# The last six inner tiles of a feed-forward's way out: four as seven half-size products in eight PSUM banks, two added onto them

## The chip, the cores and the metric

One core of a Trainium2 chip runs the kernel; the whole program is one launch. The metric is the device time of one execution in microseconds, taken as the median of several runs.

## The reference

Two layers, each a feed-forward half-step, a token mixer and a second feed-forward half-step, over 512 tokens of 1024 features in float32. The change touches the feed-forward alone. `D_FF` is 2816, which is 22 tiles of 128.

```python
def swiglu(h, w_in, w_out):
    gate, up = jnp.split(h @ w_in, 2, axis=-1)
    return (jax.nn.silu(gate) * up) @ w_out

for l in range(DEPTH):
    x = x + 0.5 * swiglu(rms_norm(x, ffn1_norm[l]), ffn1_w_in[l], ffn1_w_out[l])
    h = rms_norm(x, mix_norm[l]) @ w_mix_in[l]
    ...                      # short convolution, HGRN2, forgetting attention
    x = x + y @ w_mix_out[l]
    x = x + 0.5 * swiglu(rms_norm(x, ffn2_norm[l]), ffn2_w_in[l], ffn2_w_out[l])
```

## The kernel before

**Precision.** Every float32 product is made of three TensorE passes over `fp32r` parts: ScalarE casts the high part of an operand, VectorE subtracts it from the source for the low part, and `mm3` issues high x high, high x low, low x high. Weights go through `prepare`: ACT writes `hi` (L810), DVE writes `lo` (L812), into a buffer `hl` of which there are three. `prepare` for a step is issued `LEAD` = 3 steps before it. The moving operand is split the same way: `two`, called by `moving` for the way out (ACT L759 or L763, DVE L760 or L764; tiles `m`).

**Half-size products.** The activations stay transposed: features or inner tiles on the partitions, 512 tokens in the free dimension, cut in two halves of 256. A product of a 2x2-blocked weight with a 2x2-blocked activation is made from seven products of blocks instead of eight (P1 to P7, a scheme of the Strassen-Winograd family). Its left operands are blocks of weights and sums of blocks (S1 to S4, made by `add` and `adds`, accumulating DMAs on POOL's queue, and by `total` on DVE), its right operands blocks and sums of blocks of the activation (`SUM`, `hidden`). One product is `product()`: 24 matmuls of 128x128 weights against 256 columns into one PSUM bank.

**Way in and way out.** The way in ("I" steps) makes two inner tiles from seven products: gate and up, then SiLU on ACT, and a product on DVE into `hq`, a quarter of the hidden activation. The way out ("O" steps) takes eight inner tiles (a chunk) at a time: `CHUNKS` are tiles 0 to 7, 8 to 15 and 16 to 21. Both are woven together: `plan()` writes the order of steps `seq` from patterns of I and O, and for each step a list of jobs with ranks: loads on SP's queue, accumulations on POOL's, sums on DVE, moving operands. `halved()` runs that order; after a step's matmuls come its readout, the `prepare` of the step three further on, and the step's jobs. An engine works its instructions off in the order in which they are issued.

**The last chunk.** It goes out directly, without products: `hh` and `hl` hold the hidden tiles 16 to 21 as high and low parts (ACT L973, DVE L974), and after `halved()` the loop in `ffn` (L489 to L507) streams `w_out`'s rows against all 512 tokens, four banks for features 0 to 511 and then four for 512 to 1023: 144 matmuls of 512 columns. `stream` loads and casts those weights (`st`, L314 and L315). DVE adds each bank to the residual `xT` (L502), and `norm_part` gathers what the next norm needs (x times gain at L408 and L409, squares at L421 and L425). The fourth and last feed-forward has another end, `way_out`, which writes the output.

**PSUM.** Eight banks: `mm` 3, `sc` 2, `pt` 2, `po` 1, in two rings of four that the I steps and O steps take in turn; the rings swap at each feed-forward (`ntog`).

Of the kernel before, what the change touches and what calls it, by code (L numbers as in the profile page):

```python
# [62 lines left out]
def plan(covered):  # L63
# [5 lines left out]
    for c, pattern in ((0, "IIIIO" + "IIO" * 11 + "IOIO"), (1, "IIIIO" + "IOIIO" * 5 + "IOIOO")):  # L69
        ii, oo = iter(into(CHUNKS[c + 1])), iter(outof(c))  # L70
        seq += [next(ii if k == "I" else oo) for k in pattern]
        assert next(ii, None) is None and next(oo, None) is None
# [53 lines left out]
    for b, e, u, q in sorted(lives, key=lambda x: x[0]):  # L126
# [33 lines left out]
class Trunk:  # L160
# [297 lines left out]
    def ffn(self, w_in, w_out, next_gain, covered, begin=None, out=None):  # L458
        nc = self.nc
        tc = self.tc  # L460
        with tc.tile_pool(name=self.n("ffn"), bufs=1) as fp:
# [18 lines left out]

            f0, nf = CHUNKS[-1]
            if next_gain is not None:
                self.begin_norm(next_gain)
# [4 lines left out]
            for dg in range(2):
                banks = self.next4()  # L489

                def parts(k, kk, dg=dg):
                    r = slice((f0 + k) * P, (f0 + k + kk) * P)
                    return [w_out[r, dg * 512 : (dg + 1) * 512]]

                self.stream(
                    [(bk, slice(c, c + P), None) for bk, c in zip(banks, (0, 128, 256, 384))],
                    parts, self.last_hidden, nf,
                )
                for i in range(4):
                    j = dg * 4 + i  # L500
                    xj = self.xT[:, j, :]
                    nc.vector.scalar_tensor_tensor(  # L502
                        out=xj, in0=banks[i], scalar=0.5, in1=xj,
                        op0=ALU.mult, op1=ALU.add,
                    )
# [1417 lines left out]
```

## Time and profile before

| | us |
|---|---|
| median of 3 runs (lowest 1802.62, highest 1804.36) | 1803.07 |
| the profiled execution | 1801.38 |
| its span in the trace | 1799.6 |
| TensorE busy | 1792.0 |
| VectorE busy | 1430.1 |
| ScalarE busy | 1001.0 |
| GpSimd busy | 176.6 |

The profile is of one execution. A row of groups reads: line, engine, operation, output<-inputs with the shape of the tile, count | busy time, mean ns of one | idle time before them and what ended it. A row of the timeline reads: start in us from the span's start, duration, engine, line, operation, and in brackets the idle time before it with what ended it. Buffer numbers are left out of names.

### The profile page before, as it was taken

The page shows a single profiled execution, that of the slowest core. Times are in us where ns is not written, and L with a number is a line of the kernel's source. Part 1 is how long each engine was busy: PE and PEld are TensorE (multiplying, and loading weights), DVE is VectorE, ACT ScalarE, POOL GpSimd, SP SyncE. Part 2 cuts the span into 40 slices and gives each one's busy share as a digit, 9 for nine tenths or more (in the row PEclk, how much of TensorE's full clock was granted, in tenths as well). Part 3 has the DMA queues.
Part 4 walks back from the last instruction along what each step waited for, and adds up shares of the span by engine and source line. Part 5 has one row for each costly group of instructions (what it writes and reads, how often), then busy time and mean ns, then how long its engine had stood idle before and what let it go on. Part 6 is the DMA issues. An engine that isn't in the chain of part 4 may idle for free.

```text
span 1799.6 us, 34747 instructions
## 1 busy us (share of the span) xinstructions
PE 1792.0 (100%) x14271; PEld 1681.0 (93%) x14271; DVE 1430.1 (79%) x2006; ACT 1001.0 (56%) x1445; POOL 176.6 (10%) x184
## 2 busy tenths in 40 slices
PE   9999999999999999999999999999999999999999
PEld 7899999899888899999889999998998888999997
DVE  9889787676888798879679887876868879888793
ACT  5455554464776465556446555555547755555551
POOL 0011120100000002112001111201000000020210
PEclk9999999999999999999999999999999999999999
DMA  7659793233433857868265786913334346597762
GB/s 207 180 133 196 169 188 97 71 82 84 106 98 108 222 130 170 194 163 166 82 207 133 169 185 175 187 65 83 78 85 116 89 144 179 141 185 190 160 133 94
DMA packets 244638, 254.09 MB, mean 141 GB/s; under 512 B 18904, under 2 KB 228576, under 8 KB 244480
## 3 DMA queue, kind: packets, MB, share of 16 engines
q1 hardware_dynamic: 189424, 182.38, 33.7%
q0 software_dynamic: 54752, 69.23, 23.8%
q8 instruction: 112, 1.84, 0.4%
q14 instruction: 46, 0.38, 0.1%
q10 hardware_dynamic: 304, 0.27, 0.0%
HBM read 223.98 MB, written 2.10 MB: 126 GB/s over the span
## 4 chain that ended last, share of the span: by engine, by line
PE 94%; DVE 2%; ACT 2%; DMA 1%; issue 1%; SPq 0%; POOL 0%; ACTq 0%; DVEq 0%; POOLq 0%
PE mm L328 14%; PE mm L336 14%; PE mm L337 14%; PE sc L328 6%; PE sc L336 6%; PE sc L337 6%; PE pt L336 6%; PE pt L328 6%; PE pt L337 6%; PE po L328 4%; PE po L336 4%; PE po L337 4%; PE po L1654 1%; PE pt L1698 1%; PE pt L1352 1%
## 5 line engine op out<-in xcount | busy, mean ns | idle before, releaser
L810 ACT CAST hl<-w 128x1024 fp32r<-128x1024 f32 x322 | 336.8, 1050 | 305.9 <-PE mm L337 80.4
L812 DVE TENSOR_TENSOR hl<-w,hl 128x1024 fp32r<-128x1024 f32 x322 | 391.8, 1220 | 96.7 <-ACT hl L810 96.7
L315 DVE TENSOR_TENSOR hl<-st,hl 128x512 fp32r<-128x512 f32 (+3 forms) x196 | 162.5, 830 | 116.2 <-ACT hl L314 115.0
L314 ACT CAST hl<-st 128x512 fp32r<-128x512 f32 (+3 forms) x196 | 143.1, 732 | 174.3 <-PE po L337 66.8
L328 PE MATMUL mm<-xc,hl 128*128 128x256 f32 (+1 forms) x733 | 201.3, 276 | 0.0
L336 PE MATMUL mm<-xc,hl 128*128 128x256 f32 x728 | 201.2, 276 | 0.0
L337 PE MATMUL mm<-xc,hl 128*128 128x256 f32 x728 | 201.0, 276 | 0.0
L328 PE MATMUL sc<-xc,hl 128*128 128x256 f32 (+1 forms) x532 | 146.0, 276 | 0.0
L336 PE MATMUL sc<-xc,hl 128*128 128x256 f32 x528 | 146.0, 276 | 0.0
L337 PE MATMUL sc<-xc,hl 128*128 128x256 f32 x528 | 145.8, 276 | 0.0
L328 PEld LDWEIGHTS mm<-xc,hl 128*128 128x128 f32 x733 | 137.4, 188 | 0.2
L337 PEld LDWEIGHTS mm<-xc,hl 128*128 128x128 f32 x728 | 136.7, 188 | 0.0
L336 PEld LDWEIGHTS mm<-xc,hl 128*128 128x128 f32 x728 | 136.7, 188 | 0.0
L328 PE MATMUL pt<-xc,hl 128*128 128x256 f32 (+1 forms) x482 | 132.6, 276 | 0.0
L336 PE MATMUL pt<-xc,hl 128*128 128x256 f32 x480 | 132.6, 276 | 0.0
L337 PE MATMUL pt<-xc,hl 128*128 128x256 f32 x480 | 132.5, 276 | 0.0
L328 PE MATMUL mm<-x,hl 128*128 128x512 f32 x272 | 107.6, 396 | 0.0
L336 PE MATMUL mm<-x,hl 128*128 128x512 f32 x272 | 106.3, 391 | 0.0
L337 PE MATMUL mm<-x,hl 128*128 128x512 f32 x272 | 106.2, 390 | 0.0
L328 PEld LDWEIGHTS sc<-xc,hl 128*128 128x128 f32 x532 | 99.7, 188 | 0.2
L336 PEld LDWEIGHTS sc<-xc,hl 128*128 128x128 f32 x528 | 99.1, 188 | 0.0
L337 PEld LDWEIGHTS sc<-xc,hl 128*128 128x128 f32 x528 | 99.1, 188 | 0.0
(517 smaller groups left out, 5575.0 us busy)
## 6 DMA issues: line engine op xcount, KB each, us to landing
w<-in_ffn_w_in_dram SPq DMA_DIRECT2D x140, 512.0 KB, 5.1
w<-in_ffn_w_out_dram SPq DMA_DIRECT2D x64, 512.0 KB, 5.2
w<-in_ffn_w_out_dram POOLq DMA_DIRECT2D x56, 512.0 KB, 7.2
st<-in_w_mix_in_dram SPq DMA_DIRECT2D x88, 256.0 KB, 2.8
st<-in_ffn_w_in_dram SPq DMA_DIRECT2D x70, 256.0 KB, 3.1
w<-in_ffn_w_in_dram POOLq DMA_DIRECT2D x35, 512.0 KB, 8.9
w<-S POOLq DMA_DIRECT2D x35, 512.0 KB, 4.7
st<-in_ffn_w_out_dram SPq DMA_DIRECT2D x24, 512.0 KB, 5.3
```

The source lines that it names most:

```text
L314: a = nc.scalar.copy(hi, src[:, c : c + w])
L315: b = nc.vector.tensor_sub(lo, src[:, c : c + w], hi)
L328: i = nc.tensor.matmul(acc[:, c], ah, bh[:, c], start=first and c.start == 0, stop=False, skip_group_check=True,)
L336: nc.tensor.matmul(acc, a, b, start=False, stop=False, skip_group_check=True)
L337: i = nc.tensor.matmul(acc, c, d, start=False, stop=last, skip_group_check=True)
L810: A(nc.scalar.copy(hi, src))
L812: return lambda: V(nc.vector.tensor_sub(lo, src, hi))
L1352: nc.tensor.matmul(bank[hh][rows[par], at + x * n : at + (x + 1) * n], held[rows[hh], c * CH : (c + 1) * CH], moving(rows[hh], c), start=T ...
L1654: nc.tensor.matmul(self.ob[:, t0 + u * P : t0 + 2 * P], V[:, j, h % 4].rearrange("p a d -> p (a d)"), part[:, j, u:, :].rearrange("p i t - ...
L1698: nc.tensor.transpose(tb[:, j * P : (j + 1) * P], p[:, j * P : (j + 1) * P], self.ident)
```

## The change

In the first three feed-forwards the last chunk is cut in two. Tiles 16 to 19 become steps "o" of `plan()`: one set of seven products over all 1024 features, each of 24 matmuls of 256 columns, over two banks. Tiles 20 and 21 become two steps "T" of 48 matmuls of 256 columns, which add onto the four banks that hold the feature half r. What a product gives isn't read out into `xT` at once as in the first two chunks, but stays in the banks: P1 in `a` and, negated by an ACT copy, in `c`; P2, P5, P6, P7, P3 and P4 add on; P7's state of `a` is copied to `d`. Only P5 and P6 update `xT` on the way (L955); T0 and T1 do the rest (L966), each followed by four `norm_part`s. The hidden tiles 16 to 19 go to quarters `hq` like those of the other chunks, and only 20 and 21 to `hh` and `hl`. The order of the second half changes from `IIIIO` + 5 x `IOIIO` + `IOIOO` to `IIIIO` + 13 x `IO` + 4 x `oI` + `ooo` + `TT`. Also, the S2 sums of chunk 1's weights, accumulated by a POOL DMA before, become `total`s on DVE, as those of chunk 0 are. The fourth feed-forward keeps its order and its `way_out`.

```diff
-def plan(covered):
+def plan(covered, final):
...
+    ends = "IIIIO" + "IOIIO" * 5 + "IOIOO"
+    if not final:
+        ends = "IIIIO" + "IO" * 10 + "IO" * 3 + "oI" * 4 + "ooo" + "TT"
+    for c, pattern in ((0, "IIIIO" + "IIO" * 11 + "IOIO"), (1, ends)):
...
+        elif w[0] == 2:
+            end = {0: "P7", 1: "P3", 2: "P5", 3: "P4"}
+            m = split["P5"]
+            begin[2] = m - AHEAD_SUM - AHEAD_LOAD
+            begin[3] = split["P7"] - 2 - AHEAD_LOAD
+            when(m - AHEAD_SUM, 5, "add", u, 2, 3)
+            between(m, m + 1, "total", u, "S2")
+            when(m + 1, 6, "adds", u)
+            between(m + 2, split["P7"] - 1, "total", u, "S3")
...
-            if w[0]:
+            if w[0] and final:
                 when(split["P5"] + 1, 5, "add", u, 2, 0)
...
+    if not final:
+        n0 = {p: at["O", (2, 0), p] for p in ORDER_OUT}
+        before = [at["O", (1, 1), "P3"], at["O", (1, 1), "P4"]] + list(n0.values())
+        sums = {"P5": [(0, 1)], "P6": [(1, 1)], "P7": [], "P4": [(1, 0)]}
+        for i, p in enumerate(ORDER_OUT):
+            n = before[i]
+            for y in sums.get(p, ()):
+                when(n, 2, "hidden", 2, (0, 0), y)
+            if p == "P7":
+                when(n, 2, "hidden", 2, (0, 1), (1, 1))
+            when(n, 3, "moving", 2, p)
...
-            for dg in range(2):
-                banks = self.next4()
...
+        def last_product(u, p, banks, start):
+            hi, lo = parts.pop((u, p))
+            for n, bank in enumerate(banks):
+                for i in range(2):
+                    acc = bank[:, i * H : (i + 1) * H]
+                    if p == "T":
+                        g, t = n // 2, slice(n % 2 * H, n % 2 * H + H)
+                        xh, xl = (z[0][:, :, t] for z in (self.hh, self.hl))
+                    else:
+                        g, (xh, xl) = n, mov[2, p]
...
+        def last(n, u, p):
+            if p == "T":
+                r = u[1][1]
+                banks = [work[k][g] for g in range(2) for k in ("cb", "ad")[r]]
+            else:
+                k = {"P2": "c", "P5": "b", "P3": "b"}.get(p, "a")
+                if p == "P1":
+                    self.begin_norm(next_gain)
+                    work["c"] = [bank("O") for _ in range(2)]
+                if p in ("P1", "P5"):
+                    work[k] = [bank("I" if p == "P1" else "O") for _ in range(2)]
+                banks = work[k]
+            last_product(u, p, banks, p in ("P1", "P5"))
+            rest = prepare(*seq[n + LEAD]) if n + LEAD < len(seq) else None
+            if p == "P7":
+                work["d"] = [bank("I") for _ in range(2)]
+            for g in range(2):
+                if p == "P1":
+                    A(nc.scalar.activation(work["c"][g], banks[g], AF.Copy, scale=-1.0))
+                elif p == "P7":
+                    A(nc.scalar.copy(work["d"][g], banks[g]))
+                elif p in ("P5", "P6"):
+                    r = p == "P5"
+                    xs = self.xT[:, 4 * r + 2 * g : 4 * r + 2 * g + 2, H:]
+                    V(nc.vector.scalar_tensor_tensor(
+                        out=xs, in0=pair(banks[g]), scalar=-0.5, in1=xs, op0=ALU.mult, op1=ALU.add
+                    ))
+            if rest is not None:
+                rest()
+            if p != "T":
+                return
+            for g in range(2):
+                j = 4 * r + 2 * g
+                for b in range(2):
+                    xs = self.xT[:, j : j + 2, b * H : (b + 1) * H]
+                    nc.vector.scalar_tensor_tensor(
+                        out=xs, in0=pair(banks[2 * g + b]), scalar=0.5, in1=xs,
+                        op0=ALU.mult, op1=ALU.add,
+                    )
+                for i in range(2):
+                    self.norm_part(j + i, fp)
```

Four places show what that does to the queues; a name is a tile with its number, `hl` the parts of a weight, `m` a moving operand, `hq` a quarter of hidden tiles, `w` and `S` weights and their sums, `y`, `hh` the last hidden tiles, `xT` the residual. All are in the first feed-forward. DVE before, at the end of the products and the start of the direct stream:

```order
L812 TENSOR_TENSOR hl_3341<-w_3223,hl_3341 128x1024
L914 SCALAR_TENSOR_TENSOR xT<-pt_2876,xT 128x2x256
L812 TENSOR_TENSOR hl_3370<-w_3259,hl_3370 128x1024
L958 TENSOR_TENSOR y_3398<-g_350_3188,u_357_3252 128x2x256
L958 TENSOR_TENSOR y_3398<-g_345_3098,mm_3071 128x2x256
L315 TENSOR_TENSOR hl_3463<-st_3461,hl_3463 128x1024
L974 TENSOR_TENSOR hh_3402<-y_3398,hh_3401 128x1024
L914 SCALAR_TENSOR_TENSOR xT<-sc_2495,xT 128x2x256
L315 TENSOR_TENSOR hl_3492<-st_3490,hl_3492 128x1024
L914 SCALAR_TENSOR_TENSOR xT<-sc_2496,xT 128x2x256
```

Each step has one low part and about one readout, and the stream's weights (`st`) follow. DVE after, from the low part of I19's weights (`hl_3383`) on:

```order
L838 TENSOR_TENSOR hl_3383<-w_2971,hl_3383 128x1024
L853 TENSOR_TENSOR hq_2678<-hq_2678 128x512
L778 TENSOR_TENSOR m_3390<-hq_2678,m_3389 128x512
L838 TENSOR_TENSOR hl_3417<-w_3156,hl_3417 128x1024
L822 TENSOR_TENSOR S_3422<-w_3156,w_3154 128x1024
L838 TENSOR_TENSOR hl_3448<-w_3030,hl_3448 128x1024
L853 TENSOR_TENSOR hq_2678<-hq_2678,hq_3118 128x512
L778 TENSOR_TENSOR m_3453<-hq_2678,m_3452 128x512
L1031 TENSOR_TENSOR u_376_3419<-u_376_3419,po_3160 128x512
L838 TENSOR_TENSOR hl_3481<-S_3422,hl_3481 128x1024
L822 TENSOR_TENSOR w_3154<-S_3422,w_3351 128x1024
```

The sums of quarters and the low parts of the new moving operands (L853, L778) now stand between the low parts of the weights, beside two weight sums (L822). Directly behind them, DVE after, from the first update of `xT` for P5 to the second for P6:

```order
L955 SCALAR_TENSOR_TENSOR xT<-pt_3486,xT 128x2x256
L955 SCALAR_TENSOR_TENSOR xT<-pt_3487,xT 128x2x256
L838 TENSOR_TENSOR hl_3512<-w_3194,hl_3512 128x1024
L853 TENSOR_TENSOR hq_2678<-hq_2678,hq_3118 128x512
L774 SCALAR_TENSOR_TENSOR m_3519<-hq_2678,m_3518 128x512
L1034 TENSOR_TENSOR g_362_3315<-g_362_3315,mm_3159 128x512
L838 TENSOR_TENSOR hl_3548<-w_3154,hl_3548 128x1024
L955 SCALAR_TENSOR_TENSOR xT<-mm_3357,xT 128x2x256
L955 SCALAR_TENSOR_TENSOR xT<-mm_3358,xT 128x2x256
```

The two updates of `xT` for P6 (the last two rows) stand behind two low parts of weights, a hidden sum with its moving operand and a gate. DVE after, the last rows before the stage ends:

```order
L778 TENSOR_TENSOR m_3585<-hq_3118,m_3584 128x512
L1055 TENSOR_TENSOR y_3614<-g_362_3315,u_376_3419 128x2x256
L1055 TENSOR_TENSOR y_3614<-g_351_3187,po_3160 128x2x256
L838 TENSOR_TENSOR hl_3612<-w_3351,hl_3612 128x1024
L1071 TENSOR_TENSOR hh_3618<-y_3614,hh_3617 128x1024
L838 TENSOR_TENSOR hl_3646<-w_3522,hl_3646 128x1024
L853 TENSOR_TENSOR hq_2678<-hq_2678,hq_3118 128x512
L774 SCALAR_TENSOR_TENSOR m_3655<-hq_2678,m_3654 128x512
L838 TENSOR_TENSOR hl_3682<-w_3553,hl_3682 128x1024
```

The last sum of quarters (L853) and the low part of the last moving operand, `m_3655`, which is P4's, stand behind the low parts for y (L1071) and for T0 (`hl_3646`). ACT after, over the same stretch:

```order
L836 CAST hl_3579<-w_3229 128x1024
L778 CAST m_3584<-hq_3118 128x512
L300 ACT_TABLE_LOAD
L836 CAST hl_3612<-w_3351 128x1024
L1070 CAST hh_3617<-y_3614 128x1024
L836 CAST hl_3646<-w_3522 128x1024
L951 COPY mm_3648<-mm_3357 128x512
L951 COPY po_3649<-mm_3358 128x512
L773 ACTIVATE m_3654<-hq_2678 128x512
```

The cast of that moving operand (`m_3654`, L773) stands behind the casts for o4 (`hl_3612`), y and T0, and the two copies of P7's banks.

More of the change, by code (lines that the diff above doesn't have):

```diff
@@ L33 @@
 CHUNKS = ((0, 8), (8, 8), (16, 6))
+LAST = 20
 ORDER_IN = ("P1", "P2", "P6", "P5", "P7", "P3", "P4")
@@ L68, in plan @@
     seq = into(CHUNKS[0])
[L69 to L72, printed above, removed]
+    ends = "IIIIO" + "IOIIO" * 5 + "IOIOO"
+    if not final:
+        ends = "IIIIO" + "IO" * 10 + "IO" * 3 + "oI" * 4 + "ooo" + "TT"
+    for c, pattern in ((0, "IIIIO" + "IIO" * 11 + "IOIO"), (1, ends)):
+        of = {
+            "I": iter(into(CHUNKS[c + 1])), "O": iter(outof(c)),
+            "o": iter([("O", (2, 0), p) for p in ORDER_OUT]),
+            "T": iter([("T", (2, r), "T") for r in range(2)]),
+        }
+        seq += [next(of[k]) for k in pattern]
+        assert all(next(of[k], None) is None for k in set(pattern))
     at = {s: n for n, s in enumerate(seq)}
@@ L479, in ffn @@
                         values(n // 3, cleared)
-            f0, nf = CHUNKS[-1]
-            if next_gain is not None:
-                self.begin_norm(next_gain)
             self.ntog += 1
             if out is not None:
-                self.way_out(w_out, out, f0, nf)
-                return
-            for dg in range(2):
-                banks = self.next4()
[L491 to L505, printed above, removed]
-                    if next_gain is not None:
-                        self.norm_part(j, fp)
+                self.way_out(w_out, out, *CHUNKS[-1])
     def cover(self, fp, w_in, covered, begin, then):
@@ L789, in total @@
             q = lambda i: raw[u, i]
-            if name == "S2" and u[0] == "I":
-                sums[u] = fp.tile([P, 4, 2 * P], F32, tag="S", name=self.n("S"), bufs=2)
+            if name == "S2" and (u[0] == "I" or wide(u)):
+                sums[u] = fp.tile(shape(u), F32, tag="S", name=self.n("S"), bufs=2)
             t, a, b, op = {
@@ L832, in halved @@
         }
+        def last_product(u, p, banks, start):
[8 more added lines that the diff above has]
+                        g, (xh, xl) = n, mov[2, p]
+                    c = slice((2 * g + i) * P, (2 * g + i + 1) * P)
+                    for k in range(2):
+                        self.mm3(
+                            acc, hi[:, k, c], lo[:, k, c], xh[:, k, :], xl[:, k, :],
+                            start and i == 0 and k == 0, p == "T" and i == 1 and k == 1,
+                            False, True,
+                        )
         def product(u, p, bank, start, stop, parted):
@@ L882, in bank @@
             return self.bank(names[ring[kind]][(used[kind] - 1) % 4])
+        def last(n, u, p):
[36 more added lines that the diff above has]
+                        op0=ALU.mult, op1=ALU.add,
+                    )
+                for i in range(2):
+                    self.norm_part(j + i, fp)
         for n, (kind, w, p) in enumerate(seq):
             u = kind, w
+            if wide(u):
+                last(n, u, p)
+                run(n)
+                yield
+                continue
             new = ("P1", "P2", "P5")
@@ L891, in halved @@
                         work[("O", (w[0], g)), x] = bank(kind)
+            if u == ("I", LAST) and p == "P1" and not self.final:
+                for x in "cba":
+                    work[u, x] = bank(kind)
             if p in new and (u, k) not in work:
```

47 lines of the change are left out of this document (35 added, 12 removed).

## The prediction

> **What bounds the kernel now.** I read the page's busy shares first, then the chain that ended last, then windows laid exactly over the stage that the change rewrites and over the products before it.
>
> ```profile
> span 1799.6 us, 34747 instructions
> PE 1792.0 (100%) x14271; PEld 1681.0 (93%) x14271; DVE 1430.1 (79%) x2006; ACT 1001.0 (56%) x1445; POOL 176.6 (10%) x184
> PEclk9999999999999999999999999999999999999999
> PE 94%; DVE 2%; ACT 2%; DMA 1%; issue 1%; SPq 0%; POOL 0%; ACTq 0%; DVEq 0%; POOLq 0%
> ```
>
> TensorE is busy throughout and makes 94% of the chain, at full clock in every slice. So every matmul taken away is worth its spacing, and every wait of TensorE costs its length: nothing later gives it back. The windows (columns: stretch, its length, busy time and count of PE, PEld, DVE, ACT, POOL, then clock, DMA share, GB/s) give the spacings.
>
> ```profile
> 261.00:299.08 38.08, 38.08 (x338) 38.08 (x337) 33.70 (x36) 22.53 (x25) 2.17 (x2) 1.00 0.56 122
> 304.41:337.22 32.81, 32.81 (x146) 26.96 (x145) 17.15 (x24) 12.61 (x18) 0.00 (x0) 1.00 0.27 83
> 870.03:902.70 32.67, 32.67 (x147) 27.03 (x146) 17.79 (x23) 13.21 (x18) 0.00 (x0) 1.00 0.35 113
> 1194.61:1227.47 32.86, 32.86 (x147) 26.96 (x145) 17.15 (x25) 12.61 (x18) 0.00 (x0) 1.00 0.27 82
> ```
>
> The first row holds 14 half-size products (261.00 and 299.08 are starts of products) of 24 matmuls 256 columns wide: 38.08/14 = 2.72 us a product, 113.3 ns a matmul. The other rows are the closing stage of the first three feed-forwards, 144 matmuls of 512 columns (the counts include two or three that overlap an edge): 32.67/144 = 226.9 ns. Twice the columns, twice the time; the narrow form costs nothing extra. The second and third closing stages differ because the first and third feed-forward (32.81, 32.86) lose 0.14 and 0.19 to small waits, against the second's 32.67.
>
> The same rows show the danger. In the product stage DVE is busy 33.70 of 38.08 us; in the closing stage only 17 of 33. The change takes TensorE time out of the stage where DVE rests and puts DVE's work in.
>
> **Part 1, the products.** 96 wide matmuls for tiles 16 to 19 become 7 x 24 = 168 narrow ones; the 48 for tiles 20 and 21 become 96 narrow ones. 264 x 113.3 = 29.92 us against 144 x 226.7 = 32.64: 2.72 us less per feed-forward, 8.16 us for the three that change. The fourth keeps its path.
>
> [...]
>
> **Part 2, who feeds the products.** I call a unit of TensorE's order a step: I19 and the like for the last pair (tiles 20, 21), o1, o2, o5, o6, o7, o3, o4 for the new products, then T0 and T1. The order near the end is o1, I18 (P5), o2, I19 (P7), o5, I20 (P3), o6, I21 (P4), o7, o3, o4, T0, T1. Durations for what DVE and ACT must do:
>
> ```profile
> L810 ACT CAST hl<-w 128x1024 fp32r<-128x1024 f32 x322 | 336.8, 1050 | 305.9 <-PE mm L337 80.4 <-PE pt L337 54.6 <-PE sc L337 53.0
> L812 DVE TENSOR_TENSOR hl<-w,hl 128x1024 fp32r<-128x1024 f32 x322 | 391.8, 1220 | 96.7 <-ACT hl L810 96.7
> L315 DVE TENSOR_TENSOR hl<-st,hl 128x512 fp32r<-128x512 f32 x124 | 85.1, 688 | 62.3 <-ACT hl L314 61.1
> L314 ACT CAST hl<-st 128x512 fp32r<-128x512 f32 x124 | 76.2, 618 | 87.9 <-PE mm L337 41.2 <-PE po L337 37.4 <-DMA st<-in_w_mix_in_dram 6.8
> ```
>
> What counts in a queue is start to start, and how long a hand-over takes:
>
> ```profile
> 270.14 1.22 DVE L812 TENSOR_TENSOR hl<-w,hl 128x1024 fp32r<-128x1024 f32 x1
> 271.27 0.68 DVE L914 SCALAR_TENSOR_TENSOR xT<-sc,xT 128x512 f32<-128x512 f32 x1
> 271.87 1.21 DVE L812 TENSOR_TENSOR hl<-w,hl 128x1024 fp32r<-128x1024 f32 x1
> ...
> 277.69 0.68 DVE L922 TENSOR_TENSOR g<-g,mm 128x512 f32<-128x512 f32 x1
> 278.40 0.63 ACT L277 ACTIVATE g<-g 128x512 f32<-128x512 f32 x1 [1.59 <-DVE g L922]
> 278.94 1.04 ACT L810 CAST hl<-w 128x1024 fp32r<-128x1024 f32 x1
> ...
> 290.81 0.28 PE L328 MATMUL po<-xc,hl 128*128 128x256 f32 x1
> 291.01 1.05 ACT L810 CAST hl<-w 128x1024 fp32r<-128x1024 f32 x1 [1.66 <-PE pt L337]
> 292.09 1.23 DVE L812 TENSOR_TENSOR hl<-w,hl 128x1024 fp32r<-128x1024 f32 x1 [0.39 <-ACT hl L810]
> ```
>
> So on DVE a 1024-column operation takes 1.13 to 1.14 from start to start and a 512-column one 0.60, with its result 0.68 after its start; DVE to ACT hands over in 0.03. When a step ends (290.81 is the next one's first matmul), the cast of the weights three steps on starts 0.20 later (it needs the buffer that step held) and DVE's low part 1.08 after that. A 512-column cast takes 0.62, or 0.52 to 0.54 to the next.
>
> Now I walk DVE's queue as the order shows it, with zero at the start of I18 (steps then start at o2 2.72, I19 5.44, o5 8.16, I20 10.88, o6 13.60, I21 16.32, o7 19.04, o3 21.76, o4 24.48). The low part of I19's weights starts at 0.20 + 1.08 = 1.28. The sum of two hidden quarters for P5 follows at 2.42 and is done at 3.10; ACT casts P5's moving operand at 3.13, then o5's weights at 3.65; DVE takes their low part at 4.73.
>
> From there to the last hidden sum, the one for P4, DVE has 11 operations of 1024 columns (low parts for o5, I20, o6, I21, o7, o3, o4, T0; two weight sums; the low part of y) and 13 of 512. Twice it also waits for ACT: a moving operand's high part can only be cast when its hidden sum is done, and its low part stands next in DVE's queue, 0.68 - 0.60 + 0.03 + 0.62 + 0.03 = 0.76 idle. 11 x 1.135 + 13 x 0.603 + 2 x 0.76 + 0.07 (for y's cast) = 21.91, so P4's hidden sum starts at 26.64. TensorE wants its product at 24.48.
>
> P4's chain then ends: sum done 27.32, ACT casts 27.35 to 27.97, o4's first matmul at 28.00, the low part 28.00 to 28.69, the second matmul, which reads it, at 28.72 instead of 24.59. **Wait before o4: 4.1 us in all.** 0.7 of it is already spent at o7: its first matmul adds onto the bank that DVE must first read for P6's update of x, and that update stands behind seven 1024-column and eight 512-column operations, both ACT waits included: 4.73 + 7.95 + 4.82 + 1.52 = 19.02, done 19.70, o7 at 19.73 instead of 19.04. After 28.72 T0's operands are ready (its weights' low part 26.7, y's 25.5, before T0 at 31.2). The moves are on the path: 4.1 x 3 = 12.4 us.
>
> Were DVE's queue empty when o7 ends (21.76), the chain cast, low part, hidden sum, cast, low part would still run 0.20 + 1.08 + 1.13 + 0.71 + 0.65 + 0.72 = 4.49 against o3's 2.72 + 0.11 of cover: 1.66 us. So the wait lies between 1.7 and 4.1 unless the order is other than built; I take 4.1 since every term is a row and the count leaves DVE no gap.
>
> **Part 3, the smaller pieces.** Chunk 1's S2 sums (two a feed-forward) leave POOL's accumulating DMAs for DVE, 2 x 1.13.
>
> ```profile
> 250.00:260.00 10.00, 10.00 (x91) 10.00 (x90) 9.41 (x10) 5.81 (x7) 4.72 (x4) 1.00 1.19 215
> 260.00:270.00 10.00, 10.00 (x91) 10.00 (x90) 9.48 (x11) 5.38 (x6) 1.75 (x2) 1.00 1.17 249
> ```
>
> DVE has 0.5 to 0.6 us in ten free there, and a product's low part has some 3 us of slack (cast three steps ahead); between 0 and 2.3 per feed-forward I take 0.1, nearer nothing, because the slack is larger than one sum. In exchange the DMA share there falls.
>
> The loads: six of 512 KB replace six, plus an accumulating one from memory and one from SBUF.
>
> ```profile
> w<-in_ffn_w_out_dram SPq DMA_DIRECT2D x64, 512.0 KB, 5.2
> w<-in_ffn_w_out_dram POOLq DMA_DIRECT2D x56, 512.0 KB, 7.2
> w<-S POOLq DMA_DIRECT2D x35, 512.0 KB, 4.7
> ```
>
> The latest is the SBUF one: its sum ends at 7.1 on my scale (5.87 by the queue above, plus 1.22), so it lands near 12, and o3's cast wants it when o6 ends, at 16.3. Nothing, with 4 us of cover. On SP the new loads take the places of those removed, each issued four steps (10.9 us) before its cast: nothing, against 5.2 from issue to landing. The ACT copies of P1 (negated) and P7 into other banks cost what such copies cost today:
>
> ```profile
> L906 ACT COPY sc<-pt 128x512 f32<-128x512 f32 x4 | 2.3, 578 | 0.0
> ```
>
> Four of 0.58 sit on an engine that is 56% busy, with a whole step before the bank's next use: nothing.
>
> The way out: both halves of x now finish within the last 10.9 us, not 16 us apart, so DVE does eight updates, eight x 0.66 (gain and subtract) and seven additions for the norm beside the next stage's weights. After the first and second feed-forward what comes next uses the early features first and I take 0.1 and 0. After the third, the mixer's second bank is the one that held features 6, 7, whose update stands behind the norm work of x0 to x5. From the end of T0's third bank (4.08 + 0.20 after T0's start) DVE has six gain operations and eleven of 0.60 ahead of it:
>
> ```profile
> 320.64 0.74 DVE L409 SCALAR_TENSOR_TENSOR x<-xT,gain,x 128x512 fp32r<-128x512 f32 x1
> 321.30 0.68 DVE L425 TENSOR_TENSOR sqa<-sqa,sq 128x512 f32<-128x512 f32 x1
> 321.90 0.74 DVE L409 SCALAR_TENSOR_TENSOR x<-xT,gain,x 128x512 fp32r<-128x512 f32 x1
> ```
>
> 0.66 and 0.60 start to start: 4.28 + 6 x 0.665 + 11 x 0.603 + 0.72 = 15.6, and TensorE comes there 10.88 + 18 x 0.227 = 14.96 after T0's start. 0.6 us, once.
>
> **The sum.** -8.16 + 12.4 + 0.3 + 0.1 + 0.6 = +5.2; the closing stage's own 0.14 and 0.19 vanish: +4.9. The profiled execution took 1801.38 us (span 1799.6 and 1.8 around it), so 1806.3; the median of the three runs, 1803.07, is 1.7 above that execution, so **1808.0**, 0.27% slower. What a measurement of this kernel can tell from no change is about 0.2%, 3.6 us.
>
> **Rivals.**
> - *The wait is the short one.* DVE has caught up when o7 ends, and only P4's own chain shows: 1.66 per feed-forward, none at o7. -8.16 + 5.0 + 1.0 - 0.3 = -2.5: 1800.6, no change by that bound. For it: DVE still idles 4.4 us in the first window. Against: the count above is continuous from 4.73 on.
> - *Faster: the products hide it all.* P4's hidden sum starts by 23.1 (24.48 less 0.68 + 0.03 + 0.62 + 0.03), 3.5 earlier than counted; then o4 waits for a low part at most, and -8.16 - 0.3 leaves 1794.6. It needs DVE to pass T0's low part, or operations a sixth shorter; the order and the rows speak against both.
> - *The pause costs clock.* If TensorE, after a pause of 3 to 4 us, ran T0's first half at half speed, one step would take 5.44, +2.7 each, 1816. PEclk reads 9 in every slice of before, so no row shows what such a pause does. [...]
> - *A transfer is late.* If the SBUF accumulation took over 9 us instead of 4.7, o3 would wait by the excess: 2 us each gives 1814.
>
> **How the numbers follow.** Forecast (wait near 4.1) 0.64, its own range 1805.5 to 1810.5, about 0.08 of it below the bound of 0.2% (1806.7); short wait 0.18; all hidden 0.10; clock 0.05; transfer 0.03. Slower: 0.56 + 0.08 = 0.64; same: 0.18 + 0.08 = 0.26; faster: 0.10. The range 1800.0 to 1811.0 takes in the short wait and leaves out the last three, 0.18, and a little of the forecast's tails.
>
> **What the profile after would show.** Right: TensorE idle about 2.8 us before the first matmul of o4, released by ACT's moving cast, and 0.6 before the second, released by DVE; about 0.7 before o7, released by the update of x; products at 2.72 us; DVE without gaps but two of 0.76 in the 22 us before. Wrong: o4 starting behind o3 without a gap; narrow matmuls spaced wider than 114 ns; a granted clock under 1.0 after o4; a DMA named as releaser of a weight cast there; or, in the mixer, new waits beyond the 0.6 us.

## The result and the profile after

The changed kernel takes 1812.06 us (median of 4 runs, 1811.27 to 1813.65) against 1803.71 for the kernel before (4 runs): the ratio is 1.0052, interval 1.004 to 1.0065. It is slower, as forecast, but by 8.35 us where 5 were forecast, and 1.06 above the range. The page of the profiled execution, of 1811.27 us:

```profile
span 1809.5 us, 35556 instructions
PE 1790.4 (99%) x14631; PEld 1693.6 (94%) x14631; DVE 1473.9 (81%) x2066; ACT 1021.3 (56%) x1481; POOL 176.5 (10%) x184
PEclk9999999999999999999999999999999999999999
PE 90%; DVE 5%; ACT 2%; issue 1%; DMA 1%; SPq 0%; POOL 0%; ACTq 0%; DVEq 0%; POOLq 0%
```

TensorE is busy 1.6 us less, DVE 44 us more, and the chain that ended last gives DVE 5% where it gave 2. The clock line shows nothing: at 45 us a slice, a few microseconds at another clock don't move its digit.

**The waits.** TensorE's rows at the new products (start, duration, instruction, idle time and its releaser):

```profile
316.51 0.36 PE L360 MATMUL mm<-m,hl 128*128 128x256 f32 x1 [1.08 <-DVE xT L955]
321.92 0.28 PE L369 MATMUL pt<-m,hl 128*128 128x256 f32 x1
324.69 0.38 PE L360 MATMUL mm<-m,hl 128*128 128x256 f32 x1 [2.50 <-ACT m L773]
325.42 0.38 PE L368 MATMUL mm<-m,hl 128*128 128x256 f32 x1 [0.34 <-DVE m L774]
885.27 0.35 PE L360 MATMUL pt<-m,hl 128*128 128x256 f32 x1 [0.80 <-DVE xT L955]
893.45 0.38 PE L360 MATMUL pt<-m,hl 128*128 128x256 f32 x1 [2.29 <-ACT m L773]
1211.90 0.35 PE L360 MATMUL po<-m,hl 128*128 128x256 f32 x1 [0.80 <-DVE xT L955]
1220.08 0.58 PE L360 MATMUL po<-m,hl 128*128 128x256 f32 x1 [2.29 <-ACT m L773]
1240.50 0.47 PE L360 MATMUL mm<-x,hl 128*128 128x512 f32 x1 [0.56 <-DVE xT L966]
```

From start to start less the spacing, o4 waits 324.69 - 321.92 - 0.11 = 2.66, and its second matmul 325.42 - 324.69 - 0.11 = 0.62. The bracket before a product counts 0.16 to 0.17 less, since it begins at the end that the profile gives to the matmul before (0.28 us after its start, not 0.11); so o7 waits 1.25, 0.97 and 0.97 in the three feed-forwards, o4 2.66, 2.46 and 2.46 and then 0.62 each, and the mixer behind the third 0.73. Each stands where the prediction had it, with the releaser that it named. DVE and ACT ahead of o4:

```profile
322.16 1.22 DVE L838 TENSOR_TENSOR hl<-w,hl 128x1024 fp32r<-128x1024 f32 x1
323.29 0.68 DVE L853 TENSOR_TENSOR hq<-hq,hq 128x512 f32<-128x512 f32 x1
324.01 0.63 ACT L773 ACTIVATE m<-hq 128x512 fp32r<-128x512 f32 x1 [1.11 <-DVE hq L853]
324.67 0.69 DVE L774 SCALAR_TENSOR_TENSOR m<-hq,m 128x512 fp32r<-128x512 f32 x1 [0.70 <-ACT m L773]
```

The low part of T0's weights, P4's hidden sum, the cast, the low part: one behind the other, with DVE and ACT handing over in 0.03 to 0.04 us.

**The clock.** Windows from o4's first matmul to T0's in the three feed-forwards, and over T0 and T1 of the first (columns as in the prediction, PEclk is the third from the end):

```profile
324.69:329.75 5.06, 4.72 (x24) 4.52 (x25) 1.90 (x2) 0.88 (x1) 0.00 (x0) 0.66 0.02 3
329.75:340.63 10.88, 10.88 (x98) 10.88 (x97) 8.63 (x14) 6.20 (x11) 0.00 (x0) 1.00 0.18 48
```

```profile
893.45:896.91 3.46, 3.12 (x24) 2.92 (x25) 1.89 (x2) 0.88 (x1) 0.00 (x0) 1.00 0.00 0
1220.08:1224.74 4.66, 4.51 (x24) 4.22 (x25) 1.90 (x2) 0.88 (x1) 0.00 (x0) 0.64 0.01 4
```

o4's 24 matmuls and their 0.62 of wait should take 3.34. The second feed-forward takes 3.46 at full clock, the first 5.06 and the third 4.66 at 0.66 and 0.64: 1.60 and 1.20 us more than the second. That is what the sum had left out, and the prediction had named a clock under 1.0 behind o4 as a sign that it is wrong. All four runs have a mean clock of 0.998. In the trace the granted clock is 0.50 from 325.72 to 329.13 and from 1220.01 to 1223.42, 3.41 us each time, and 1.00 on both sides. Why two of three equal pauses, and for how long, shows in windows of that length laid so that one ends where the slow matmuls end (329.07):

```profile
322.24:325.66 3.42, 0.63 (x3) 0.43 (x4) 2.48 (x4) 2.22 (x4) 0.00 (x0) 1.00 0.00 0
325.66:329.07 3.41, 3.41 (x18) 3.41 (x18) 1.17 (x1) 0.00 (x0) 0.00 (x0) 0.51 0.02 5
...
888.86:892.27 3.41, 2.29 (x20) 2.09 (x18) 3.41 (x4) 2.79 (x4) 0.00 (x0) 1.00 0.01 2
892.27:895.68 3.41, 1.89 (x14) 1.70 (x15) 2.38 (x3) 1.56 (x2) 0.00 (x0) 1.00 0.00 0
...
1216.54:1219.95 3.41, 1.25 (x11) 1.04 (x9) 2.82 (x3) 2.30 (x5) 0.00 (x0) 1.00 0.00 0
1219.95:1223.36 3.41, 3.14 (x13) 2.84 (x14) 1.92 (x2) 1.01 (x2) 0.00 (x0) 0.51 0.02 5
```

One grid fits both ends: 1223.36 - 329.07 = 894.29 = 262 x 3.4133 (261 windows would have 3.426 us, 263 would have 3.400). The granted clock itself falls 0.06 us behind these boundaries, at 325.72 and 1220.01, also 894.29 apart. Here a window in which TensorE is busy 0.63 or 1.25 us is followed by one at half clock (0.51); in the second feed-forward the same pause falls over a boundary, leaves 2.29 and 1.89 busy, and costs no clock.

### The profile page after: what moved, and what is told of

Read it like the earlier page. It is cut to its first block, busy times and chain, and to the rows that moved or that the text cites. A ratio compares the mean times of both kernels' runs of the same rounds, so it can differ in the third digit from the quotient of the medians.

```text
span 1809.5 us, 35556 instructions
## 1 busy us (share of the span) xinstructions
PE 1790.4 (99%) x14631; PEld 1693.6 (94%) x14631; DVE 1473.9 (81%) x2066; ACT 1021.3 (56%) x1481; POOL 176.5 (10%) x184
## 4 chain that ended last, share of the span: by engine, by line
PE 90%; DVE 5%; ACT 2%; issue 1%; DMA 1%; SPq 0%; POOL 0%; ACTq 0%; DVEq 0%; POOLq 0%
PE mm L360 13%; PE mm L368 13%; PE mm L369 13%; PE sc L368 6%; PE sc L360 6%; PE sc L369 6%; PE pt L368 6%; PE pt L360 6%; PE pt L369 6%; PE po L368 3%; PE po L369 3%; PE po L360 3%; DVE hl L838 1%; PE po L1751 1%; PE pt L1795 1%
## 5 line engine op out<-in xcount | busy, mean ns | idle before, releaser
L836 ACT CAST hl<-w 128x1024 fp32r<-128x1024 f32 x346 | 362.0, 1049 | 336.3 <-PE mm L369 92.7
L838 DVE TENSOR_TENSOR hl<-w,hl 128x1024 fp32r<-128x1024 f32 x346 | 422.1, 1223 | 104.9 <-ACT hl L836 104.9
L347 DVE TENSOR_TENSOR hl<-st,hl 128x512 fp32r<-128x512 f32 (+2 forms) x178 | 140.7, 791 | 82.4 <-ACT hl L346 81.4
L360 PE MATMUL mm<-xc,hl 128*128 128x256 f32 (+1 forms) x717 | 196.8, 276 | 0.0
L368 PE MATMUL mm<-xc,hl 128*128 128x256 f32 x712 | 196.8, 276 | 0.0
L369 PE MATMUL mm<-xc,hl 128*128 128x256 f32 x712 | 196.6, 276 | 0.0
L346 ACT CAST hl<-st 128x512 fp32r<-128x512 f32 (+2 forms) x178 | 124.1, 699 | 127.2 <-PE mm L369 52.6
L368 PE MATMUL sc<-xc,hl 128*128 128x256 f32 x512 | 141.6, 276 | 0.0
L369 PE MATMUL sc<-xc,hl 128*128 128x256 f32 x512 | 141.3, 276 | 0.0
L368 PE MATMUL pt<-xc,hl 128*128 128x256 f32 x496 | 137.0, 276 | 0.0
L369 PE MATMUL pt<-xc,hl 128*128 128x256 f32 x496 | 136.9, 276 | 0.0
L360 PEld LDWEIGHTS mm<-xc,hl 128*128 128x128 f32 x717 | 134.4, 188 | 0.2
L369 PEld LDWEIGHTS mm<-xc,hl 128*128 128x128 f32 x712 | 133.7, 188 | 0.0
L368 PEld LDWEIGHTS mm<-xc,hl 128*128 128x128 f32 x712 | 133.7, 188 | 0.0
L360 PE MATMUL mm<-m,hl 128*128 128x256 f32 x400 | 111.5, 279 | 3.6 <-ACT m L773 2.5
L368 PE MATMUL mm<-m,hl 128*128 128x256 f32 x400 | 111.4, 278 | 0.4 <-DVE m L774 0.3
L369 PE MATMUL mm<-m,hl 128*128 128x256 f32 x400 | 111.2, 278 | 0.0
```

What stands on the lines that cost most here:

```text
L346: a = nc.scalar.copy(hi, src[:, c : c + w])
L347: b = nc.vector.tensor_sub(lo, src[:, c : c + w], hi)
L360: i = nc.tensor.matmul(acc[:, c], ah, bh[:, c], start=first and c.start == 0, stop=False, skip_group_check=True,)
L368: nc.tensor.matmul(acc, a, b, start=False, stop=False, skip_group_check=True)
L369: i = nc.tensor.matmul(acc, c, d, start=False, stop=last, skip_group_check=True)
L836: A(nc.scalar.copy(hi, src))
```

## Experiments

Theory A: the 3 us missing from the sum are half clock set off by the pause, and the pauses are DVE's queue, so a different order or less work on DVE removes both. Rivals: B, the slow matmuls belong to o4 or to its late operand, not to the pause; C, the pause is DVE's and only moves; D, the narrow products have a price of their own. Medians stand beside those of the kernel before on the same chip; ratios with intervals. What an experiment changes, it changes in the first three feed-forwards.

### Order: T0 ahead of o4 (e1)

```diff
-ends = "IIIIO" + "IO" * 10 + "IO" * 3 + "oI" * 4 + "ooo" + "TT"
+ends = "IIIIO" + "IO" * 10 + "IO" * 3 + "oI" * 4 + "ooToT"
```

> One letter of the order moves: T0 (tiles 20, 21 onto the banks of features 0 to 511) goes ahead of o4, so the end is o7, o3, T0, o4, T1. P4's moving operand gets one step of 5.44 us more. If the wait before o4 is P4's late chain, and the half clock behind it only follows from that pause, then both go: of the waits there stays the one before o7 (about 1.0 each), some 0.3 before T0's second matmul, and about 1 more at the way into the mixers: 3 x 3.1 less, minus 1, and 2.9 of half clock less: about 11 us under the changed kernel, 1800 to 1802, and no row at half clock. Rival: the pause is a pause of DVE as such and moves to T0, whose operands are prepared in the same queue: then 2 to 3 us of wait stand before T0 instead and the time stays within 3 us of 1812.

1803.18 (10 runs) against 1802.24: 1.0008, 0.9998 to 1.0017. The pause before o4 is gone, T0 waits at most 0.28, and the granted clock is 1.000. That is A and not C: two letters' exchange takes back nearly all that the change had lost. It is 1 to 3 us short of the expectation, and the profile shows one place: in the second feed-forward a matmul of chunk 1 came 0.18 late (at 818.25), and from there on the spacing was not 113.3 ns (a window ahead of it and one behind it, with their matmul counts, which include those that overlap an edge):

```profile
793.00:815.00 22.00, 22.00 (x196) 22.00 (x195) 18.57 (x20) 11.00 (x12) 3.47 (x3) 1.00 0.64 141
821.00:888.00 67.00, 66.95 (x568) 66.77 (x568) 57.27 (x65) 37.01 (x44) 5.63 (x5) 1.00 0.60 145
```

67.00/568 = 118 ns at clock 1.00; from start to start the rows have 117 to 119, 117.8 on average, steady for 70 us, 2.6 us lost. The same late matmul stands in the first and the third feed-forward (252.91 and 1143.42), and there the spacing stays at 113.3.

### Less work on DVE, same order (e2)

```diff
-if p == "P7": when(n, 2, "hidden", 2, (0, 1), (1, 1))     # and the sum for P5 likewise
+when(at P1 and P2, 4, "hidden_dma", ...)   # shortened; it calls nc.gpsimd.dma_start(x, y, accum_op=ALU.add)
```

> The sums of quarters for P5 and for P7 become accumulating DMAs on POOL's queue, issued two to four steps earlier; the order is that of the changed kernel. DVE has two operations of 512 columns less (1.2 us) and one hand-over to ACT less (0.7). If DVE's backlog sets both waits, the wait before o7 (1.25, 0.97, 0.97) goes to about zero and that before o4 falls only by what is left over (to about 2.5 + 0.6), since P4's chain stands where it stood: 3 us less in all at the full clock. The half clock may or may not stay, since the pause is hardly shorter: 1806 to 1809. If the wait before o7 is another cause (the bank, the clock), it stays at 1 us.

1811.44 (4 runs) against 1802.24: 1.0048, 1.0031 to 1.0065; above its expectation. The wait before o7 is gone in all three feed-forwards, so it was DVE's backlog. Before o4 stay 2.33 + 0.61, 2.81 + 0.61 and 2.79 + 0.62. By the rows the waits are 2.8 us shorter than in the changed kernel, but the time isn't. In the profiled execution, the longest of the four (1813.82), the clock takes a part of that. Windows on this execution's grid:

```profile
890.83:894.24 3.41, 0.98 (x9) 0.78 (x7) 2.90 (x3) 2.29 (x4) 0.00 (x0) 1.00 0.00 0
894.24:897.65 3.41, 3.06 (x12) 2.77 (x13) 1.92 (x2) 1.09 (x2) 0.00 (x0) 0.50 0.00 0
897.65:901.06 3.41, 3.41 (x18) 3.41 (x17) 0.00 (x0) 0.52 (x1) 0.00 (x0) 0.50 0.00 0
1218.51:1221.92 3.41, 1.77 (x16) 1.58 (x14) 3.41 (x4) 2.60 (x4) 0.00 (x0) 1.00 0.00 0
```

The second feed-forward is slow for two windows: the first slow one still held 0.8 us of waits. The third, with nearly the same pause, has 1.77 busy in its window and stays at full clock. There was also a stretch of 117.8 ns, from 253.7 to 322.9, 2.6 us. The three other runs (1811.08 to 1811.76) have the changed kernel's mean clock, 0.998; what takes the gain there isn't shown.

### Pauses by themselves (e3, e4, e5)

On the order of e1 with e2's DMAs; DVE gets needless copies, T1 waits.

```diff
+if p == "P3":
+    for _ in range(next(IDLE)): nc.vector.tensor_copy(t[:, 0], t[:, 0])   # t: a quarter no longer used
 if rest is not None: rest()                                              # low part of T1's weights
```

> For the clock alone: the order of e1 with the two sums off DVE (so that next to no other wait is left), and ahead of the low part of T1's weights DVE gets 6, 7 and 6 needless copies of 256 columns in the first, second and third feed-forward. By the queue TensorE should pause for about 1.6 us before the mixer's first matmuls in the first, 1.0 before the third matmul of T1 in the second, 2.3 before the mixer in the third. If the half clock needs a pause of 2.5 us or more, no row is at half clock: matmuls after the pause at 113 ns (227 for 512 columns). If any pause does it, or if the narrow products themselves draw the clock down, there are rows at 213 (or 427) ns here too.

> As e3, with 8, 8 and 9 copies: pauses of about 2.6, 3.1 and 3.5 us before the third matmul of T1, without a second gap behind them. If the pause is the cause, then the longer ones (3.1 and 3.5) are followed by some 3.4 us at 213 ns a matmul, that is 16 matmuls at 100 ns more, 1.6 us, the same for both lengths; 2.6 may go either way. If the half clock came from P4's product or its late operand, nothing happens here, since T1 reads operands that have long been ready but for its weights' low part.

> As e4, with 9, 10 and 12 needless copies on DVE ahead of the low part of T1's weights. In e4 the pauses came out at 1.15, 1.93 and 2.20 us, 1.2 to 1.5 under the count, and no matmul behind them was slow; so here some 2.3, 3.2 and 4.7 us. If a pause beyond about 3 us halves the clock, the third (and perhaps the second) is followed by matmuls of 256 columns at 213 ns for some 3.4 us, and the first is not. Rival: the half clock belongs to the product that waits for its moving operand; then none here, whatever the length.

The pauses came out shorter than counted, since DVE takes the updates of x in between: in e3 0.67 and 1.46 before the mixers and 0.09 in the second feed-forward, in e4 1.15, 1.93 and 2.20, in e5 2.26, 2.95 and 4.10 before T1's third matmul. The longest of e3 and of e4:

```profile
1227.08 0.47 PE L365 MATMUL mm<-x,hl 128*128 128x512 f32 x1 [1.30 <-DVE xT L979]
```

```profile
1223.15 0.38 PE L374 MATMUL po<-hh,hl 128*128 128x256 f32 x1 [2.04 <-DVE hl L843]
```

None in e3 and e4 is followed by a slow matmul; the mean clock of both runs is 1.000. In e5 the last two are (windows on the grid through 904.49; 1232.17 - 904.49 = 327.68 = 96 x 3.4133):

```profile
331.05:334.46 3.41, 1.70 (x14) 1.70 (x15) 3.10 (x6) 0.61 (x2) 0.00 (x0) 1.00 0.34 80
334.46:337.88 3.42, 3.42 (x33) 3.42 (x32) 3.42 (x6) 1.87 (x4) 0.00 (x0) 1.00 0.26 73
897.66:901.08 3.42, 1.19 (x10) 1.19 (x11) 3.42 (x7) 2.75 (x5) 0.00 (x0) 1.00 0.54 152
901.08:904.49 3.41, 3.41 (x19) 3.41 (x18) 3.41 (x6) 0.70 (x2) 0.00 (x0) 0.52 0.53 158
1225.34:1228.76 3.42, 0.16 (x1) 0.16 (x2) 3.39 (x7) 2.83 (x6) 0.00 (x0) 1.00 0.37 87
1228.76:1232.17 3.41, 3.41 (x17) 3.41 (x18) 2.92 (x5) 0.56 (x1) 0.00 (x0) 0.52 0.18 63
```

This settles A against B: T1's product, whose operands had long been ready but for the weights' low part, is slowed just as o4 was. After 899.89 TensorE even ran ten matmuls at full clock before the boundary at 901.08: the granted clock is 1.00 from 899.90 to 901.20 and 0.50 from 901.40 to 904.40. Single runs: 1801.80, 1803.34 and 1810.32.

### The S2 sums (e6, e7, e8)

e6 is the changed kernel with one S2 sum of chunk 1 back on POOL; e8 is e1's order with e2's DMAs; e7 is e8 with e6's line.

```diff
-            if w[0] and final:
+            if w[0] and (final or w[1]):
                 when(split["P5"] + 1, 5, "add", u, 2, 0)
```

> The changed kernel, with one of the two S2 sums of chunk 1 given back to an accumulating POOL DMA. In the changed kernel one product of chunk 1 in each of the three feed-forwards starts its second matmul 0.18 to 0.19 us late (252.70, 821.74, 1148.37), where before there was no such gap. By the count of DVE's queue the gap goes: 0.5 us in all. If such a gap is also what lets the spacing go to 117.8 ns for many products (as in the second feed-forward of e1, from 817.97 on, and in the first of e2), that form doesn't show ahead of the closing stage here, and the spread of the runs is smaller. The waits before o7 and o4 and the half clock stay: 1810 to 1812.

> T0 ahead of o4, the sums for P5 and P7 off DVE, one S2 sum back on POOL. By the count no wait is left in the products, before o7, T0 or o4, and only about 0.9 on the way into each mixer. If the matmuls saved are worth what their spacing says, 8.2 us, and nothing else is lost: 1803 - 8.2 - 0.4 + 2 = 1796 to 1798 at the median, no row at half clock, none at 117.8 ns. If the narrow products have a price of their own that the waits only hid, it stays at 1800 or above.

> As e7, with both S2 sums on DVE as in the changed kernel, so that the gap of 0.18 us in one product of each feed-forward is back. If the gap costs only itself, 0.5 us more than e7. If it now and then sets off the spacing of 117.8 ns, that lasts until the next pause, and since there is none before the mixer here, up to 25 products at 0.1 us, 2.7 us in a feed-forward where it happens: the median 1 to 4 us above e7 and the runs further apart.

e6: 1814.95 (4 runs) against 1802.75: 1.0069, 1.0051 to 1.0086; above its expectation. The gap of 0.18 us is gone, but in the third feed-forward another stands in its place, a low part late by 0.72.

```profile
1157.14 0.38 PE L369 MATMUL mm<-xc,hl 128*128 128x256 f32 x1 [0.55 <-DVE hl L838]
```

Its profile is of the one run without half clock, 1811.15, though its pauses before o4 are as long as the changed kernel's (3.07, 3.26 and 3.26 in all); the three others have a mean clock of 0.996 to 0.997 and take 1813.14 to 1817.51.

e7: 1800.65 (11 runs), 0.9989, 0.998 to 0.9998. e8: 1799.50 (10 runs), 0.998, 0.9971 to 0.9989, both against 1802.75. So the sum back on POOL didn't help, contrary to the expectation; both versions beat the kernel before. e7 is 2.7 us above its range and inside the range of its rival, that the narrow products have a price of their own (the part on Part 1 below comes back to it). e7's profile has a gap of 0.14 in the first feed-forward, at 262.08, and from there to the mixer 117.8 ns again, 2.9 us:

```profile
263.00:337.00 74.00, 74.00 (x631) 74.00 (x630) 64.09 (x76) 42.82 (x55) 6.04 (x6) 1.00 0.49 122
```

In e8's profile the gap of 0.17 is there in all three feed-forwards (252.84, 817.44, 1140.02), and none is followed by 117.8 ns. Neither of the two cases that its expectation had, 0.5 or 1 to 4 us above e7, came.

### P4 sooner, same order (e9)

```diff
-n = before[i]
+n = n0["P6"] if p == "P4" else before[i]     # and two moving operands of 2 x 256 share a buffer of 4 x 256
```

> The changed kernel with two moving operands in one buffer (they are half as wide as the buffer), so that P4's no longer waits for P7's to be used, and P4's sum and split issued two steps sooner, with P3's. Order and everything else as in the changed kernel. By the count of DVE's queue the wait before o4 goes from 2.5 + 0.6 to one wait of some 1.9 us, that before o7 stays at 1.0: 1.2 less each, 3.6 us. No pause up to 2.3 us was followed by half clock (e3, e4, e5), five of nine of 2.9 to 3.4 were, so the half clock should go as well, 2.9 us in the profiled execution: 1804 to 1807, with a granted clock of 1.000 in every run. If the pause's length is not what matters, the clock stays at 0.998 and the time at 1808 to 1810.

1805.80 (8 runs) against 1802.12: 1.0021, 1.001 to 1.0031, inside its range. The wait before o4 is one of 1.61 or 1.62, and the clock full behind it:

```profile
324.21 0.39 PE L360 MATMUL mm<-m,hl 128*128 128x256 f32 x1 [1.45 <-ACT mm L954]
```

```profile
324.30:328.30 4.00, 4.00 (x35) 4.00 (x36) 2.44 (x3) 1.94 (x3) 0.00 (x0) 1.00 0.02 4
```

The mean clock is 1.000 in seven of the eight runs and 0.999 in one. By the rows the waits before o7 and o4 are 5.0 us shorter than in the changed kernel, and the 2.8 us of half clock are gone; of these 7.8 us the medians show 4.7 (3.7 above the kernel before in place of 8.35). Where the rest went isn't shown.

### S3 off DVE, and S2 in other steps (e10, e11)

```diff
-            between(m + 2, split["P7"] - 1, "total", u, "S3")
+            when(m + 1, 5, "add", u, 0, 2)                                   # e10, on e8
-                between(split["P5"] + 1, split["P5"] + 2, "total", u, "S2")
+                between(split["P5"] + 1 + w[1], split["P5"] + 1 + w[1], ...)  # e11, on e10, chunk 1 only
```

> e8, and the second weight sum of the new products (S3) becomes an accumulating POOL DMA from memory: 1.13 us of DVE less in the stretch before T0. By the count the wait before T0 (0.56, 0.28, 0.29) and the second one on the way into the mixers (0.35, 0.68) go, and most of 0.95: 2 to 2.5 us less than e8, 1797 to 1798. If the DMA lands late, o7 waits for its weights instead and nothing is gained.

> e10, with the two S2 sums of chunk 1 set one step apart on DVE (the first a step after P5's split, the second two) where the planner had put them at two steps that left one moving operand 0.18 us late. By the count no matmul of the products waits any longer. If the spacing of 117.8 ns starts only behind a short gap (in e10 from 1140.4 to 1223.8, right behind the gap at 1140.16; the same in e1 and e2; in e7 behind one of 0.14), no such stretch is in the profile, and the median comes out 0.6 (the three gaps) to 2 us under e10, with a smaller spread: 1796.5 to 1798.5. If the spacing comes and goes by itself, stretches of it show without a gap ahead, and the spread stays at 7 us.

e10: 1799.22 (11 runs, 1795.81 to 1802.84) against 1802.12: 0.9981, 0.9973 to 0.999; above its expectation. The waits went as counted, all but 0.95 before the first mixer's norm, yet the median is hardly below e8's. The profile has one reason: from a matmul at 1140.16, 0.18 late, to the end of the stage the spacing is 117.8 ns, which costs 3.2 us:

```profile
1141.00:1223.00 82.00, 82.00 (x699) 82.00 (x698) 70.72 (x82) 47.02 (x60) 8.86 (x9) 1.00 0.61 138
```

e11: 1798.33 (11 runs, 1797.18 to 1801.34) against 1802.25: 0.9977, 0.9968 to 0.9986, the fastest median, and inside its range. But it isn't without gaps: a low part comes 0.15 late in each feed-forward (261.30, 827.03, 1152.02). Behind the first two the spacing is 117.8 to the end of the stage (the second is shown), behind the third 113.3:

```profile
828.00:902.00 74.00, 74.00 (x631) 74.00 (x630) 64.22 (x75) 43.83 (x55) 7.15 (x7) 1.00 0.55 133
```

Its profile is of one of its three longest runs, 1801.27; the eight shortest take 1797.18 to 1798.83. Whether such a spacing comes without a gap e11 can't tell, since it has gaps.

### Many gaps (e12)

```diff
+if n % 8 == 5 and not self.final:
+    for _ in range((4,6,8,5,7,9,6,8,10)[n // 8 % 9]): nc.vector.tensor_copy(t, t)   # 256 columns
```

> For the spacing alone: e11 with 4 to 10 needless copies of 256 columns on DVE ahead of the low part of the weights at every eighth step of the first three feed-forwards, which by the count gives some 25 gaps of 0.1 to 4 us before the second or third matmul of a product. If a short gap can set off 117.8 ns, several of the stretches behind these gaps have it, others 113.3, and each stretch keeps its spacing until the next gap. If the long product stretches of e1, e2, e7 and e10 had another cause, all stretches here stay at 113.3. A pause of 4 us, if one comes out that long, should be followed by half clock.

One run, 1824.51. Behind a gap of 0.20 at 662.45 the spacing is 117.8 for 12 us, behind one of 0.17 at 730.31 it is 113.3; the same in other places. Two things speak against the gap as the only cause: at 106.50 the slow spacing begins with no start more than 0.01 us late, 8 us behind the last gap, and at 674.70 and 1006.4 it goes back to 113.3 with no pause. Three pauses, of 2.01, 2.35 and 3.03, are followed by half clock; the two shorter on this execution's grid:

```profile
276.34:279.76 3.42, 1.57 (x14) 1.38 (x13) 3.32 (x7) 0.65 (x2) 0.00 (x0) 1.00 0.20 52
279.76:283.17 3.41, 3.41 (x18) 3.41 (x17) 3.40 (x5) 1.49 (x2) 0.00 (x0) 0.51 0.76 261
829.30:832.72 3.42, 1.41 (x12) 1.42 (x13) 3.42 (x4) 0.22 (x1) 1.32 (x2) 1.00 0.22 34
832.72:836.13 3.41, 3.41 (x19) 3.41 (x18) 3.41 (x4) 1.32 (x2) 1.24 (x1) 0.51 1.16 168
```

So 2.01 us were enough here where 2.26 in e5 were not: 1.57 us busy in the window against 1.70. In the profiles of the changed kernel, e2, e5 and e12 half clock followed nine windows that were themselves at full clock, the busiest of them with 1.57 us busy. The least busy ones that it didn't follow are in e4 and e6. Neither has half clock before TensorE has stopped for good, but then the granted clock falls, at 1799.82 and 1810.42, and that gives the grid (1799.82 - 1222.96 = 169 x 3.4133, 1810.42 - 1219.91 = 173 x 3.4133; in the changed kernel it falls so at 1810.52, 590.51 = 173 x 3.4133 behind 1220.01). The longest pause of e4:

```profile
1219.55:1222.96 3.41, 1.57 (x14) 1.37 (x13) 3.41 (x8) 1.10 (x2) 0.00 (x0) 1.00 0.23 62
1222.96:1226.37 3.41, 3.22 (x28) 3.22 (x29) 3.41 (x7) 2.41 (x5) 0.00 (x0) 1.00 0.29 75
```

Its pause of 1.93 leaves 1.65 busy, and two pauses of e6 before o4 leave 1.60; all stay at full clock. So in these runs the edge lies at about 1.57 us busy of 3.41, a little under half a window: half clock followed that in e12 and not in e4.

## Why the prediction was wrong

**Part 1 held.** T0 and T1 take 10.88 us for 96 matmuls, 113.3 ns each: 2.72 us per feed-forward saved, 8.16 in all, as summed. One sign that the prediction had named as wrong did come, a spacing wider than 114 ns: behind the wait at o7, o7 and o3 run at 117.8 ns in the second and third feed-forward, 0.2 us each. D, a price of the narrow products' own, is out for e8's profiled execution, which has no such stretch in its products: there the three feed-forwards, from the first product to the first matmul behind T1, are 5.8 us shorter than before. Of the 8.5 us expected (8.16, and 0.33 of the old stage's small waits) the S2 gaps and the waits before T0 and the third mixer take 2.3. That the whole execution is only 3 us shorter lies in the mixers, which are 0.9 and 1.9 us longer there. The long stretches at 117.8 ns stay open: the feed-forward of the kernel before shows none, in its one profile, but its mixers run at that spacing for 10 us each (455.30 to 465.56 in the first).

**Part 2, the waits, held.** 12.4 us were summed for o7 and o4. Measured are 3.2 before o7 and 7.6 + 1.9 before o4, 12.6. Within that, o7 waits 0.3 to 0.6 more than the walk had and o4 0.2 to 0.4 less. The first has a row in DVE's queue of the first feed-forward:

```profile
306.14 0.69 DVE L778 TENSOR_TENSOR m<-hq,m 128x512 fp32r<-128x512 f32 x1 [1.02 <-ACT m L778]
```

DVE stood 1.02 us there for ACT's cast, where the walk had 0.76; why the cast came so late wasn't followed up. e2 showed the backlog as the cause of the wait at o7, e1 and e9 that P4's place in the queue sets the one at o4.

**The step that failed is the clock, which the sum put at nothing.** It was the third rival, "the pause costs clock", at 2.7 us each and a chance of 0.05; no row of before held a pause, so both were the author's estimates. No run shows the 2.7: in the profiled execution the clock costs 1.60, 0 and 1.20 us, 2.8 in all. The price was too high, since the granted clock is 0.50 for one window of 3.41 us and not for the 5.44 of a whole step, and the chance far too low: what decided in these runs is not the length of the pause (2.01 us were enough in e12, 2.26 in e5 were not), but how much of a window of 3.413 us on a fixed grid is busy, and a pause of 3.3 with one matmul in it can lie in one so that 0.63 or 1.25 us are busy. That the grid is fixed shows in the 262 and 96 whole windows between two ends; the clock was back at full after one slow window in eight of nine cases; and a window busy for 1.57 us of 3.41 was idle enough in e12. So a pause of 3.3 us can halve the clock or not, by where the boundary falls: two of three did in the profiled execution, which is chance.

**Part 3.** The S2 sums cost 0.18 us at one matmul and 0.11 at the next, 0.29 per feed-forward and not 0.1; the third mixer's wait was 0.73 and not 0.6; no load was late, and the ACT copies hid, as said. By the timelines, again from the first product to the first matmul behind T1, the first feed-forward is 3.73 us longer than before (2.72 and 0.16 of the old stage's small waits less; 0.29, 1.33 around o7, 2.66, 0.62, 0.12 and 1.60 more: 3.74), the second 1.99, the third 3.03. That is 8.75 of the 9.9 us between the two profiled executions. The third feed-forward's mixer comes out 1.7 longer, of which the named wait is 0.73; what runs ahead of the first product and the first mixer are 0.3 shorter each. What moves there is not followed up, and the kernel before alone spreads by 3 to 5 us from run to run.

**The ranges of the rivals.** "Short wait" and "all hidden" didn't come: DVE's queue was as full as counted. The range stopped at 1811 because the clock's case was left out of it as one of the small ones; with half clock behind two or three of the three pauses, at the 1.4 us each that the profile shows on average, the forecast would have been 1808 + 2.8 to 4.2.

## To carry to other kernels

Where a change lets TensorE wait for two microseconds or more, count the clock with it: lay the wait over windows of 3.413 us. In these runs a full-clock window ahead of half clock had at most 1.57 us busy of it, and the slow one behind it cost another 1.20 or 1.60 us in the changed kernel. A wait that came from an operation's place in DVE's queue was cheaper to move than to shorten here: T0 and o4 add onto their banks in either order (e1 has T0 first), so the product whose operand comes last can go last, and that exchange alone was worth 7 us here (8.35 above the kernel before became 0.94). And once the long waits are out, look at the spacing behind gaps of 0.15 us too: six stretches that lost 2.6 to 3.2 us each began right behind one, though most such gaps were followed by none.

## Of the hardware, not expected

- Half clock set in at the boundary of a window, not at the pause's end: in e5 ten matmuls ran at full clock between 899.89 and 901.08, with 1.00 granted up to 901.20 and 0.50 from 901.40 on. It lasted one window in eight cases, in which the slow window itself was 3.14 us busy or more, and two windows in the second feed-forward of e2, where the first slow one was 3.06 busy. Slow matmuls of 256 columns stood 213 ns apart (in the changed kernel 15 of them take the 3.20 us from 325.77 to 328.97).
- In these profiles the matmuls of 256 columns have two steady spacings at clock 1.00, 113.3 (T0 and T1: 96 in 10.88 us) and 117.8 ns (e1 behind 818.25) from start to start. Six long stretches of the slower one in the products (e1, e2, e7, e10, e11 twice; up to 84 us, 2.6 to 3.2 us lost each time) begin right behind a gap of 0.14 to 0.18 us before the second or third matmul of a product. The same gap often isn't followed by one (three of three in the changed kernel, in e8 and in e9), and e12 shows it beginning without a gap and ending without a pause. What makes the difference between the two is open. It may be why e8, e10 and e11, whose counted waits differ by 2 us, lie within 1.2 us of each other, and why the runs of one kernel spread as they do (e10 by 7.0 us, e11 by 4.2).
